# Weight residues of every fourth block by an adding transfer from HBM

## The chip, the cores and the metric

The kernel runs on one core of a Trainium2 chip. The metric is the device time of one execution in microseconds (us); lower is better.

## What is computed

The reference is one layer of a retention network with its MLP, for one sequence of 256 tokens, width 2048, all in float32:

```python
x = x + retention_mixer(rmsnorm(x, norm1), w_in, gain, w_out)     # 8 heads, DK = 256, DV = 512
x = x + square(relu(rmsnorm(x, norm2) @ w_up)) @ w_down           # width 8192
return rmsnorm(x, final_norm)

# the mixer: q, k, v, g = split(h @ w_in); q and k turned by rotary angles
# o = (q k^T * decay) v, chunk by chunk; y = head_norm(o) * silu(g) @ w_out
```

Nearly all the work is in products of activations with weights: w_in is 2048 x 12288, w_out 4096 x 2048, w_up 2048 x 8192, w_down 8192 x 2048, 268 MB in all. Each weight is read once.

## The kernel before

TensorE multiplies float32r numbers, which keep fewer bits than float32. So each weight w is split into two parts, `wh` (w rounded to float32r) and `wl = w - wh` (the residue), and so is each activation; a product is three passes, wh·xh + wl·xh + wh·xl, added up in PSUM.

Weights lie in HBM in contiguous blocks of 1 MB, 128 partitions by 2048 floats. `load_block` (L49) fetches one: a transfer on SP's queue into a `raw` tile (three buffers, L50 to L52), then for each of two halves of 1024 columns a cast to `wh` on ScalarE (L59) and a subtraction to `wl` on VectorE (L60). `wh` and `wl` have four buffers each (L55, L56), so the halves of two blocks. A half is two row tiles of 512 columns in w_qk, w_v, w_g and w_up, 1 row tile of 1024 columns in w_o and w_down. The first projection loads its four blocks row tile by row tile instead, with activations ahead of each (`lead`).

There are 256 blocks in this order. For each of 8 heads: gates (w_g, 4 blocks), queries and keys (w_qk, 4), values (w_v, 4). Then the output projection w_o in two halves of 16 blocks. Then twice (the MLP's two halves in width): w_up in 8 groups of 4 blocks, w_down in two halves of 16 blocks. `proj_cols` (L74) has weights stationary and is used for w_qk and w_up: a 512-column matmul with `wh` (L82) and a 256-column one with `wl` (L83). `proj_rows` (L89) has activations stationary and is used for the rest: per row tile, token block and 512 columns three matmuls of 512 columns (L97 with `wh`, L98 with `wl`, L101 with `wh`). In the last half of w_down the last four row tiles (the last two blocks) are kept and multiplied at the end, one accumulator after another (`late=4`, L116 to L127).

Other work of a head is put between blocks as fillers: `mix` of the head before (L268) and its `turn` (L294) behind the second block of gates and of queries, `scores` (L248) behind the second block of values. `mix` ends in a power on POOL (`rsqrt`, L141) for each token block. POOL has little else: sums of squares of x at the start, the transfers of x (L325) and of final_norm, the powers of the other norms.

Each engine works through its instructions in its own order. What the program's builder puts first is not always what the code names first: the casts of later blocks stand ahead of the work that waits for earlier matmuls.

Of the kernel before, what the change touches and what calls it, by code (L numbers as in the profile page):

```python
# [9 lines left out]
F32 = mybir.dt.float32  # L10
F32R = mybir.dt.float32r
AF = mybir.ActivationFunctionType
ALU = mybir.AluOpType
PSUM = bass.MemoryType.PSUM

P = 128
T = 256
D = 2048
# [7 lines left out]
EPS = 1e-6  # L26
# [3 lines left out]

@with_exitstack
def trunk_kernel(ctx: ExitStack, tc: tile.TileContext, io, out):
    """One retention layer and its squared-ReLU MLP.

    Every weight product is three float32r passes over exact 12-bit parts (w = wh + wl,
    x = xh + xl): wh*xh + wh*xl + wl*xh, accumulated in float32.
    """
    nc = tc.nc

    cp = ctx.enter_context(tc.tile_pool(name="cp", bufs=1))  # L40
# [3 lines left out]
    def bank(name):  # L44
        return ps.tile([P, 512], F32, tag="bank", name=name)

    # ---- weights: a block of 1 MiB, loaded whole and split in two halves; or, row tile by
    # row tile, with lead(row tile) before each ----
    def load_block(src, rows, cols, lead=None):  # L49
        raw = wp.tile([P, 2048], F32, tag="raw", name="raw", bufs=3)  # L50
        if lead is None:
            nc.sync.dma_start(raw, src)  # L52
        parts = []
        for s in range(2):
            wh = wp.tile([P, 1024], F32R, tag="wh", name="wh", bufs=4)  # L55
            wl = wp.tile([P, 1024], F32R, tag="wl", name="wl", bufs=4)  # L56
            r = raw[:, s * 1024 : (s + 1) * 1024]
            if lead is None:
                nc.scalar.copy(wh, r)  # L59
                nc.vector.tensor_sub(wl, r, wh.bitcast(F32))  # L60
            for k in range(rows // 2):
                sl = slice(k * cols, (k + 1) * cols)
                if lead is not None:
                    row = s * rows // 2 + k
                    lead(row)
                    nc.sync.dma_start(r[:, sl], src[:, row * cols : (row + 1) * cols])
                    nc.scalar.copy(wh[:, sl], r[:, sl])  # L67
                    nc.vector.tensor_sub(wl[:, sl], r[:, sl], wh[:, sl].bitcast(F32))  # L68
                parts.append((wh[:, sl], wl[:, sl]))
        return parts  # L70

    # weights stationary: acc[o][n, t] (xh) and acc[o][n, T + t] (xl) over the rows of w,
    # o = 0..3 blocks of 128 columns
    def proj_cols(src, xs, accs, fillers=()):  # L74
        for g in range(KT // 4):
            parts = load_block(src[g], 4, 512)
            for j, (wh, wl) in enumerate(parts):
                kt = 4 * g + j
                for o, acc in enumerate(accs):
                    c = slice(o * P, (o + 1) * P)  # L80
                    both = xs[:, kt].rearrange("p a t -> p (a t)")
                    nc.tensor.matmul(acc, wh[:, c], both, start=(kt == 0), stop=False)  # L82
                    nc.tensor.matmul(acc[:, :T], wl[:, c], xs[:, kt, 0, :], start=False, stop=(kt == KT - 1))  # L83
            for f in [f for at, f in fillers if at == g]:
                f()

    # activations stationary: accs[b][c][t, n] over nk row tiles, two token blocks; the last
    # `late` row tiles go to one accumulator after another, with done(b, c) behind each
    def proj_rows(blocks, per, xs, accs, nk, after=(), late=0, done=None, lead=None):  # L89
        nch = len(accs[0])  # L90
        kept = []
# [26 lines left out]
                if done:  # L118
                    done(b, c)

# [1 line left out]
    xs = cp.tile([P, KT, 2, T], F32R, tag="xs", name="xs")  # L122
    xr = cp.tile([P, KT, T], F32, tag="ys", name="xr", padded_shape=[P, VT * 2, T])
    norm1 = cp.tile([P, KT], F32, name="norm1")
# [6 lines left out]
    nc.vector.memset(ones, 1.0)  # L131
    nc.vector.memset(mhalf, -0.5)

    # while the first loads are under way: the activation table, and the tensor engine's clock
    warm = cp.tile([P, 1], F32, name="warm")
    nc.scalar.activation(warm, ones[:, 0:1], AF.Silu)
    pw = bank("pw")
# [1 line left out]
        nc.tensor.matmul(pw[:, :P], ones, ones, start=True, stop=True)  # L139

    def rsqrt(r, v):  # L141
        """r = v ** -0.5 for [P, 1] tiles."""
        nc.gpsimd.tensor_tensor(r, v, mhalf, op=ALU.pow)

    def split_scaled(dst, src, scale):
        """dst[:, 0] + dst[:, 1] = src * scale, scale [P, 1]."""
        nc.scalar.activation(dst[:, 0, :], src, AF.Copy, scale=scale)
        nc.vector.scalar_tensor_tensor(
            dst[:, 1, :], src, scale, dst[:, 0, :].bitcast(F32), op0=ALU.mult, op1=ALU.subtract
        )  # L150

    with tc.tile_pool(name="ap", bufs=1) as ap:
        # x transposed, times norm1, in two parts; sums of squares by token
        sq = ap.tile([P, 4, T], F32, name="sq")
        sqs = ap.tile([P, T], F32, name="sqs")
        cosr = ap.tile([P, T], F32, name="cosr")
# [3 lines left out]
        def load_x(k0, n):  # L160
            ks = slice(k0, k0 + n)
            nc.sync.dma_start(xr[:, ks], io["xT"][:, ks])
            for k in range(k0, k0 + n):
                split_scaled(xs[:, k], xr[:, k], norm1[:, k : k + 1])

        def lead_x(k):
            """x ahead of the first weights: row tile by row tile, then four at once."""
            if k < 4 or k % 4 == 0:
                load_x(k, 1 if k < 4 else 4)

# [30 lines left out]
            nc.vector.tensor_mul(cosr, cosr, rsrow)  # L201
            nc.vector.tensor_mul(sinr, sinr, rsrow)

# [1 line left out]
        st = {}  # L205

        def gates(h, after, lead=None):
# [38 lines left out]
            st["v"] = v  # L246

        def scores(h):  # L248
            """Decayed scores, keys on partitions: columns 0..255 keys 0..127, 256..383 keys 128..255."""
            qk = st["qk"]  # L250
            pst = bank("pst")
            for b in range(NB):
                q = slice(b * P, T)
                to = slice(0, T) if b == 0 else slice(T, T + P)
                for i in range(2):
                    nc.tensor.matmul(
                        pst[:, to], qk[:, 1, i, b * P : (b + 1) * P], qk[:, 0, i, q], start=(i == 0), stop=(i == 1)
                    )
            sd = ap.tile([P, 384], F32, tag="sd", name="sd")
            sh = ap.tile([P, 384], F32R, tag="sh", name="sh")  # L260
            sl = ap.tile([P, 384], F32R, tag="sl", name="sl")
            nc.vector.tensor_mul(sd[:, :T], pst[:, :T], dec[:, h])
            nc.vector.tensor_mul(sd[:, T:384], pst[:, T:384], dec[:, h, :P])
            nc.scalar.copy(sh, sd)
            nc.vector.tensor_sub(sl, sd, sh.bitcast(F32))
            st["s"] = sh, sl
# [49 lines left out]
                nc.sync.dma_start(dec, io["dec"])  # L316
            values(h, [(1, lambda h=h: scores(h))])

# [1 line left out]
        acc0 = [[bank("acc_o") for _ in range(2)] for _ in range(NB)]  # L320
        proj_rows(io["w_o"][0], 2, ys, acc0, VT, [(1, lambda: mix(H - 1)), (4, lambda: turn(H - 1))])

# [1 line left out]
    x = mp.tile([P, NB, D], F32, name="x")  # L324
# [4 lines left out]
    ms2 = mp.tile([P, NB], F32, name="ms2")  # L329
# [10 lines left out]
        )  # L340

    def partial_sum(b):
        """ms2 = the first three sums + D * EPS"""
        m = ms2[:, b : b + 1]
        nc.vector.tensor_scalar(m, ss[:, b, 0:1], ss[:, b, 1:2], D * EPS, op0=ALU.add, op1=ALU.add)
        nc.vector.tensor_add(m, m, ss[:, b, 2:3])
# [40 lines left out]
            nc.tensor.matmul(psr[:, b * P : (b + 1) * P], ones, dg2[:, b], start=True, stop=True)  # L387
        nc.vector.tensor_copy(rsrow2, psr[:, :T])

# [1 line left out]
    fnorm = mp.tile([P, D], F32, name="fnorm")  # L391
    nc.gpsimd.dma_start(fnorm, io["final_norm"])
    rs3 = mp.tile([P, NB], F32, name="rs3")
# [21 lines left out]
    for fh in range(2):  # L415
        hs = cp.tile([P, VT, 2, T], F32R, tag="ys", name="hs")
        for c in range(8):
            acc = [bank("acc_u") for _ in range(4)]
            proj_cols(io["w_up"][8 * fh + c], x1s, acc, [(1, second_norm)] if fh == 0 and c == 0 else ())
            for o in range(4):  # L420
                t = mp.tile([P, T], F32, tag="t", name="t", bufs=3)
                s = mp.tile([P, T], F32, tag="s", name="s", bufs=3)
# [7 lines left out]
        for half in range(2):  # L430
            acc = [[bank("acc_d") for _ in range(2)] for _ in range(NB)]
            last = fh == 1
            proj_rows(
                io["w_down"][fh][half], 2, hs, acc, VT,
                late=4 if last and half == 1 else 0,
                done=(lambda b, c: finish(b, half, c)) if last else (lambda b, c: add_residual(acc, half, b, c)),
# [1 line left out]


def _tables():  # L440
    """Rotary and decay tables: functions of the shapes alone."""
    f = np.float32
    inv = f(10000.0) ** (-np.arange(0, DK, 2, dtype=f) / f(DK))
    ang = np.arange(T, dtype=f)[None, :] * inv.astype(f)[:, None]
    cos, sin = np.cos(ang).astype(f), np.sin(ang).astype(f)
    lg = np.log1p(-np.exp2(-5.0 - np.arange(H, dtype=np.float64)))
    j, i = np.arange(P)[:, None], np.arange(T)[None, :]
    seen = (j // CHUNK) <= (i // CHUNK)
    dist = np.abs(i - j)
    dec = np.exp(lg[None, :, None] * dist[:, None, :]) * seen[:, None, :] * DK**-0.5  # L450
    return cos, sin, np.ascontiguousarray(dec.astype(f))


def _blocks(w, rows, cols):
    """[K, N] -> [N / cols, K / (128 rows), 128, rows, cols], each block contiguous."""
    k, n = w.shape
    w = w.reshape(k // (P * rows), rows, P, n // cols, cols).transpose(3, 0, 2, 1, 4)
    return np.ascontiguousarray(w).reshape(n // cols, k // (P * rows), P, rows * cols)
# [44 lines left out]
```

## Time and profile before

| | |
|---|---|
| median of 2 runs | 1492.38 us (1492.07 to 1492.69) |
| span of the profiled execution | 1491.0 us |
| TensorE (PE) busy | 1471.6 us, 99% |
| VectorE (DVE) busy | 852.9 us, 57% |
| ScalarE (ACT) busy | 675.8 us, 45% |
| GpSimd (POOL) busy | 40.3 us, 3% |
| read from HBM | 275.09 MB, 186 GB/s over the span |
| mean granted TensorE clock | 0.994 |

PE is a matmul, PEld a weight load on TensorE. A wait is written as the engine, line and tile that waited, an arrow, and what ended the wait. In a timeline, the figure in square brackets is the idle time of the engine before the instruction and what ended it. "SPq" and "POOL ... DMA_DIRECT2D" are issues of transfers. Ends of matmuls are modelled, so their starts are used for rates. A granted clock of 1.00 is 2.4 GHz, 0.50 is 1.2 GHz.

### The profile page before, as it was taken

To read this page: it belongs to the slowest core of one execution; us is meant where nothing else is said; L and a number is where in the kernel's file an instruction comes from. 1 tells how busy PE (TensorE), PEld (TensorE's weight loads), DVE (VectorE), ACT (ScalarE), POOL (GpSimd) and SP (SyncE) were. 2 spreads that over 40 slices of the span, in tenths; PEclk is the share of its full clock that TensorE was granted. 3 is DMA by queue.
4 is the path that set the end of the run, shared out by engine and by line. 5 is a ranking of instruction groups with operands and counts; after the bars stand their busy time and mean duration, and the time that the engine had idled before them with its cause. 6 is when DMAs were issued, how large, how long until landed. Compare 5 with 4: busy or idle time off the path is not lost.

```text
span 1491.0 us, 17881 instructions
## 1 busy us (share of the span) xinstructions
PE 1471.6 (99%) x7172; PEld 1233.2 (83%) x7172; DVE 852.9 (57%) x1099; ACT 675.8 (45%) x870; POOL 40.3 (3%) x48
## 2 busy tenths in 40 slices
PE   7999999999999999999999999999999999999997
PEld 5888888888888888888888888888888888888885
DVE  8656565656565656546466566544446566554645
ACT  5444444444444444434345455533334555443332
POOL 6000000000000000000000000000000000000000
PEclk8999999999999999999999999999999999999999
DMA  6654454454445445655555555555555555555552
GB/s 235 225 187 182 170 198 170 170 188 179 173 174 191 172 174 191 254 198 175 192 175 192 178 189 190 181 194 196 192 185 189 194 176 195 180 189 195 198 185 98
DMA packets 42260, 278.35 MB, mean 187 GB/s; under 512 B 5056, under 2 KB 5952, under 8 KB 9408
## 3 DMA queue, kind: packets, MB, share of 16 engines
q1 hardware_dynamic: 41616, 274.05, 52.2%
q0 software_dynamic: 416, 3.15, 0.5%
q8 instruction: 56, 0.92, 0.2%
q14 instruction: 28, 0.23, 0.0%
q10 hardware_dynamic: 144, 0.01, 0.0%
HBM read 275.09 MB, written 2.10 MB: 186 GB/s over the span
## 4 chain that ended last, share of the span: by engine, by line
PE 96%; DVE 1%; DMA 1%; issue 1%; ACT 0%; POOL 0%; SPq 0%; POOLq 0%; ACTq 0%; DVEq 0%
PE acc_u L82 16%; PE acc_qk L82 8%; PE acc_u L83 8%; PE acc_d L101 8%; PE acc_d L97 8%; PE acc_d L98 8%; PE acc_qk L83 4%; PE acc_v L101 4%; PE acc_v L97 4%; PE acc_v L98 4%; PE acc_o L97 4%; PE acc_o L101 4%; PE acc_g L101 4%; PE acc_o L98 4%; PE acc_g L98 4%; PE acc_g L97 4%
## 5 line engine op out<-in xcount | busy, mean ns | idle before, releaser
L60 DVE TENSOR_TENSOR wl<-raw,wh 128x1024 fp32r<-128x1024 f32 x504 | 615.6, 1224 | 600.9 <-ACT wh L59 600.8
L59 ACT CAST wh<-raw 128x1024 fp32r<-128x1024 f32 x504 | 529.8, 1051 | 703.6 <-PE acc_d L101 204.4
L82 PE MATMUL acc_u<-x1s,wh 128*128 128x512 f32 x1024 | 362.1, 398 | 0.0
L83 PE MATMUL acc_u<-x1s,wl 128*128 128x256 f32 x1024 | 287.8, 281 | 0.0
L82 PEld LDWEIGHTS acc_u<-x1s,wh 128*128 128x128 f32 x1024 | 192.5, 188 | 47.4
L97 PE MATMUL acc_d<-wh,hs 128*128 128x512 f32 x512 | 200.0, 391 | 0.0
L98 PE MATMUL acc_d<-wl,hs 128*128 128x512 f32 x512 | 199.9, 390 | 0.0
L83 PEld LDWEIGHTS acc_u<-x1s,wl 128*128 128x128 f32 x1024 | 192.2, 188 | 0.0
L82 PE MATMUL acc_qk<-xs,wh 128*128 128x512 f32 x512 | 182.1, 398 | 0.0
L101 PE MATMUL acc_d<-wh,hs 128*128 128x512 f32 x512 | 160.8, 393 | 0.0
L83 PE MATMUL acc_qk<-xs,wl 128*128 128x256 f32 x512 | 143.9, 281 | 0.0
L82 PEld LDWEIGHTS acc_qk<-xs,wh 128*128 128x128 f32 x512 | 96.3, 188 | 23.1
L98 PEld LDWEIGHTS acc_d<-wl,hs 128*128 128x128 f32 x512 | 96.1, 188 | 22.2 <-DVE wl L60 0.3
L101 PEld LDWEIGHTS acc_d<-wh,hs 128*128 128x128 f32 x512 | 96.2, 188 | 20.8
L97 PEld LDWEIGHTS acc_d<-wh,hs 128*128 128x128 f32 x512 | 96.2, 188 | 20.4
L98 PE MATMUL acc_g<-wl,xs 128*128 128x512 f32 x256 | 101.9, 398 | 7.5 <-DVE wl L68 7.5
L97 PE MATMUL acc_g<-wh,xs 128*128 128x512 f32 x256 | 101.9, 401 | 0.5 <-ACT wh L67 0.5
L101 PE MATMUL acc_g<-wh,xs 128*128 128x512 f32 x256 | 102.1, 399 | 0.0
L97 PE MATMUL acc_v<-wh,xs 128*128 128x512 f32 x256 | 100.8, 394 | 0.0
L101 PE MATMUL acc_v<-wh,xs 128*128 128x512 f32 x256 | 100.6, 393 | 0.0
L97 PE MATMUL acc_o<-wh,ys 128*128 128x512 f32 x256 | 100.6, 393 | 0.0
L98 PE MATMUL acc_o<-wl,ys 128*128 128x512 f32 x256 | 100.0, 391 | 0.0
(96 smaller groups left out, 1279.5 us busy)
## 6 DMA issues: line engine op xcount, KB each, us to landing
raw<-in_w_up SPq DMA_DIRECT2D x64, 1024.0 KB, 4.9
raw<-in_w_down SPq DMA_DIRECT2D x64, 1024.0 KB, 4.9
raw<-in_w_qk SPq DMA_DIRECT2D x32, 1024.0 KB, 4.9
raw<-in_w_v SPq DMA_DIRECT2D x32, 1024.0 KB, 4.9
raw<-in_w_o SPq DMA_DIRECT2D x32, 1024.0 KB, 4.9
raw<-in_w_g SPq DMA_DIRECT2D x28, 1024.0 KB, 4.9
raw<-in_w_g SPq DMA_DIRECT2D x16, 256.0 KB, 6.3
x<-in_x POOLq DMA_DIRECT2D x1, 2048.0 KB, 10.4
```

The costliest lines, as they stand in the source:

```text
L59: nc.scalar.copy(wh, r)
L60: nc.vector.tensor_sub(wl, r, wh.bitcast(F32))
L82: nc.tensor.matmul(acc, wh[:, c], both, start=(kt == 0), stop=False)
L83: nc.tensor.matmul(acc[:, :T], wl[:, c], xs[:, kt, 0, :], start=False, stop=(kt == KT - 1))
L97: nc.tensor.matmul(accs[b][c], xs[:, kt, 0, t], wh[:, n], start=(kt == 0), stop=False)
L98: nc.tensor.matmul(accs[b][c], xs[:, kt, 0, t], wl[:, n], start=False, stop=False)
L101: nc.tensor.matmul(accs[b][c], xs[:, kt, 1, t], wh[:, n], start=False, stop=(kt == nk - 1))
```

## The change

Every fourth call of `load_block` (the counter is raised in each call), unless it is one with `lead`, makes `wl` in another way. ScalarE writes a sign-turned copy of `raw` into `wl`; since `wl` is float32r, that copy is rounded as `wh` is, so it is -wh. Then a transfer on POOL's queue reads the same half of the block from HBM a second time and adds it onto `wl`, which becomes w - wh. VectorE's subtraction is left out there. The halves of the other blocks, the matmuls, buffers and loads stay. The diff also drops comments (not shown).

```diff
+    count = [0]
+
     def load_block(src, rows, cols, lead=None):
+        count[0] += 1
+        by_dma = lead is None and count[0] % 4 == 0
         raw = wp.tile([P, 2048], F32, tag="raw", name="raw", bufs=3)
         if lead is None:
             nc.sync.dma_start(raw, src)
...
             r = raw[:, s * 1024 : (s + 1) * 1024]
             if lead is None:
                 nc.scalar.copy(wh, r)
-                nc.vector.tensor_sub(wl, r, wh.bitcast(F32))
+                if by_dma:
+                    nc.scalar.activation(wl, r, AF.Copy, scale=-1.0)
+                    nc.gpsimd.dma_start(out=wl, in_=src[:, s * 1024 : (s + 1) * 1024], accum_op=ALU.add)
+                else:
+                    nc.vector.tensor_sub(wl, r, wh.bitcast(F32))
```

## Rows read from the trace of the kernel before

**Rows 1.** Page, engine totals (busy us, share, instructions) and chain that ended last.

```profile
PE 1471.6 (99%) x7172; PEld 1233.2 (83%) x7172; DVE 852.9 (57%) x1099; ACT 675.8 (45%) x870; POOL 40.3 (3%) x48
...
PE 96%; DVE 1%; DMA 1%; issue 1%; ACT 0%; POOL 0%; SPq 0%; POOLq 0%; ACTq 0%; DVEq 0%
```

**Rows 2.** List of waits: who waited for whom, us in total, times, longest us.

```profile
DVE wl L60 <- ACT wh L59: 600.8, 439, 2.3
...
PE acc_g L98 <- DVE wl L68: 7.5, 3, 4.0
...
PEld acc_d L98 <- DVE wl L60: 0.3, 1, 0.3
```

**Rows 3.** Timeline of TensorE and ScalarE, values of head 4: start, duration, instruction.

```profile
347.72 0.39 PE L97 MATMUL acc_v<-wh,xs 128*128 128x512 f32 x1
...
355.97 0.39 PE L97 MATMUL acc_v<-wh,xs 128*128 128x512 f32 x1
...
356.21 1.05 ACT L59 CAST wh<-raw 128x1024 fp32r<-128x1024 f32 x1 [1.69 <-PE acc_v L101]
```

**Rows 4.** Groups by line: busy us, mean ns of one, idle before, releaser.

```profile
L60 DVE TENSOR_TENSOR wl<-raw,wh 128x1024 fp32r<-128x1024 f32 x504 | 615.6, 1224 | 600.9 <-ACT wh L59 600.8
L59 ACT CAST wh<-raw 128x1024 fp32r<-128x1024 f32 x504 | 529.8, 1051 | 703.6 <-PE acc_d L101 204.4 <-PE acc_u L82 157.3 <-PE acc_o L101 102.2
```

**Rows 5.** Timeline of ScalarE and POOL around mix, in the gates behind head 3.

```profile
311.39 1.05 ACT L59 CAST wh<-raw 128x1024 fp32r<-128x1024 f32 x1 [1.70 <-PE acc_g L101]
...
315.39 0.72 ACT L291 ACTIVATE y<-y,rv 128x512 f32<-128x512 f32 x1 [2.96 <-DVE mv L285]
...
315.79 0.55 POOL L143 TENSOR_TENSOR rv<-ve,mhalf 128x1 f32<-128x1 f32 x1 [0.46 <-DVE ve L286]
```

**Rows 6.** Issue of x on POOL, and 615 to 616 (engines' busy us, PEclk, DMA, GB/s).

```profile
614.72 0.90 POOL L325 DMA_DIRECT2D x<-in_x  x1 [15.07 <-ACT ys L147]
...
615.00:616.00 1.00, 1.00 (x6) 0.80 (x5) 1.00 (x3) 0.05 (x2) 1.00 (x2) 1.00 0.00 0
```

**Rows 7.** One block's load: issue on SP, and stretches of its traffic (columns as rows 6).

```profile
321.35 0.33 SPq L52 DMA_DIRECT2D raw<-in_w_qk  x1
...
321.50:323.00 1.50, 1.50 (x8) 1.24 (x7) 0.17 (x1) 1.05 (x1) 0.00 (x0) 1.00 0.53 98
...
326.00:327.50 1.50, 1.50 (x11) 1.31 (x10) 1.23 (x1) 0.43 (x2) 0.00 (x0) 1.00 0.00 0
```

**Rows 8.** Transfers: the load queue's packets, MB and share; KB each, us to landing.

```profile
q1 hardware_dynamic: 41616, 274.05, 52.2%
...
raw<-in_w_down SPq DMA_DIRECT2D x64, 1024.0 KB, 4.9
...
x<-in_x POOLq DMA_DIRECT2D x1, 2048.0 KB, 10.4
```

**Rows 9.** Chain of work in order of time: TensorE's other work in the heads.

```profile
358.88 1.31 PE pst L256 x8
382.18 2.07 PE po L279 x9
406.54 0.87 PE pt L301 x8
```

**Rows 10.** Timeline of TensorE at the start, and stretches there (columns as rows 6).

```profile
10.58 0.50 PE L98 MATMUL acc_g<-wl,xs 128*128 128x512 f32 x1 [1.04 <-DVE wl L68]
...
28.46 0.51 PE L98 MATMUL acc_g<-wl,xs 128*128 128x512 f32 x1 [2.52 <-DVE wl L68]
...
29.98 0.63 PE L98 MATMUL acc_g<-wl,xs 128*128 128x512 f32 x1
...
33.38 0.39 PE L97 MATMUL acc_g<-wh,xs 128*128 128x512 f32 x1
...
12.00:14.00 2.00, 1.98 (x8) 0.97 (x6) 2.00 (x4) 2.00 (x5) 1.84 (x3) 1.00 1.03 409
...
31.00:33.00 2.00, 2.00 (x7) 1.52 (x6) 2.00 (x3) 0.65 (x1) 1.34 (x2) 0.50 0.24 45
```

## The prediction

> **What bounds the kernel now.** I read the page's engine totals and the chain of work that ended last first. The reader is to see that TensorE is busy for 99% of the span and makes up 96% of the chain [rows 1]: whatever makes it wait is added to the time, and work taken from another engine gives nothing back. Next the list of waits: TensorE's only waits for weight residues are 7.5 us in the first blocks and 0.3 us in a half of w_down [rows 2]. VectorE waits 600.8 us for ScalarE's casts [rows 2], and a cast waits 1.69 us for TensorE to give back a buffer [rows 3]; both engines have room. So the question is one of lateness alone: does the new transfer deliver `wl` before TensorE asks for it?
>
> **The time it has.** `wh` and `wl` have four buffers each, and a block uses two. A half that TensorE finishes gives its buffers to the half four further on, which TensorE reaches after the three halves between. In the values of head 4, 36 matmuls (three halves) take 355.97 - 347.72 = 8.25 us, so a half is 2.75 us and a matmul 0.229 us [rows 3]. The cast that wants the freed buffer starts 0.24 us later (356.21) [rows 3]. Cast and subtraction need 1.05 and 1.22 us [rows 4]: `wl` is there 2.5 us after the buffer comes free, 5.7 us early.
>
> **What goes and what comes.** The counter reaches 256 (w_qk, w_v, w_g and w_o 32 blocks each, w_up and w_down 64 each). The fourth is a `lead` block, so blocks 8, 12, ... 256 change: 63, with 126 halves. In each projection of four blocks that is the last one; in each half of w_o and w_down it is every fourth of 16.
> - VectorE loses 126 x 1.22 = 154 us, with no effect on the end: it waits more than that already [rows 2].
> - ScalarE gains 126 sign-turned copies. I price them by the cast, which has their shape: 126 x 1.05 = 132 us [rows 4]. A cast and a copy (2.1) fit into a half (2.75). What hides them is ScalarE's wait for TensorE's buffers [rows 3]; without it each would push the next cast by 1.05 us, still within 5.7.
> - `raw` is released 2.1 us behind the start of the cast, not 2.3, so the load that waits for it on SP's queue may start 0.2 us sooner. Nothing: `raw` has a third buffer.
> - POOL gets 126 issues, each waiting for its copy. Behind them in its queue stand only the small powers of the norms. Casts of block 3 of w_g, which the code places behind `mix`, already run ahead of it (311.39, before `y` at 315.39), so I take it that the issues do as well. If instead they stood behind the powers of `mix`, which end at 315.79 + 0.55 = 316.3 [rows 5], about 2.4 us before TensorE wants that block, some 3.5 us would be lost in each of 8 mixes: 28 us.
> - The queue gains 126 transfers of 512 KB. Here lies the cost.
>
> **The price of one transfer.** Nothing in the trace accumulates, so I bound it. *Start:* x's issue on POOL at 614.72 lasts 0.90 us, and the DMA engines carry nothing from 615 to 616 [rows 6]; I take first traffic at 1.4 us behind the issue. A load that SP issues at 321.35 averages 98 GB/s from 321.5 on [rows 7]; I take 0.5 us for it. *Work:* 274.05 MB keep 16 engines busy for 52.2% of 1491 us [rows 8], so a block of 1.05 MB takes 2.98 us of them. An add needs the old contents of `wl` too: 512 KB written stand for 0.5 MB read (1.49 us) if the second read is free, or for 1 MB read (2.98 us) if it goes through the same engines. *End:* the load of rows 7 carries its last bytes before 326 and lands at 321.35 + 4.9 = 326.25 [rows 7, 8]; I take 0.6 us. *From above:* x, 2 MB from POOL with loads beside it, lands after 10.4 us [rows 8]. I take 2.98 us, since the old contents must come from somewhere, and the nearest transfer of as many bytes read is a block's load.
>
> The Trainium skill ("Collectives: The Full Stack", section "The bandwidth ceiling: the fold count and why AG ≠ RS ≠ AR") says that an adding transfer is slower by its two source reads and not by its arithmetic. No run here shows that yet.
>
> **The sum.** Put the buffer of the block's first half free at 0. Cast and copy end at 0.24 + 2.1 = 2.3, POOL starts at 2.4, traffic starts at 3.8, 2.98 us of work end at 6.8, and the landing is at 7.4: 0.8 us ahead of 8.25. The second half is 2.75 us later, and the next block's load, released at 5.05, brings traffic from 5.6. From there the first transfer runs at half rate (1.2 us left, until 8.0, landed 8.6: up to 0.4 late). At 6.55, when the second starts, 0.7 (first) + 2.5 (load) + 2.98 = 6.2 us of work are queued; it ends near 12.5 and lands near 13.1, where TensorE wants it at 2.75 + 8.25 = 11.0. **Late by 2.1 us**; the first half's 0.4 is within that, as it moves the second's need along.
>
> By stage: w_o, w_down and w_up, 39 blocks without the last: 39 x 2.1 = 82. In the heads TensorE does other work between the blocks ahead: 1.31 us of scores, 2.07 of mix, 0.87 of turn [rows 9]. That leaves 0.8 in w_v (8 blocks, 6), nothing in w_g (7) and 1.2 in w_qk (8, 10). In the last block rows 28 to 31 are kept for the end: behind row 26, TensorE has only row 27 and six matmuls (2.75 + 1.37 = 4.1 us) before it wants the first half, which lands at 7.4: 3.3 late. The second half lands near 10.4 for a need at 8.1: 2.3 more, so 6 in all. Sum of waits: 82 + 6 + 10 + 6 = 104 us.
>
> **TensorE's clock.** After the wait of 2.52 us at the start matmuls come at 2.4 GHz at first, then the granted clock is 0.50 (1.2 GHz) between 31 and 33, though TensorE is busy [rows 10]. From 29.98 to 33.38 [rows 10] eight matmuls came 0.425 apart, not 0.229: 1.6 us lost. After the wait of 1.04 us the clock stays at 1.00 [rows 10]. A wait of 2.1 lies between; I charge half of 1.6 to each of the 39 blocks with about 2 us, 31 us. The bounds are 0 and 62. Against this execution: 1491 + 104 + 31 = 1626 in span, and 1.4 us more for the median (1492.4 against 1491.0): **1627 us**.
>
> **Rivals.**
> 1. *Hidden: not slower.* The old contents are read beside the stream, so a transfer has 1.49 us of work. Traffic from 3.8, at half rate beside a load 3.0 us, landing 7.4 against 8.25; the second half no later relative to its need. Only the last block waits, 2 to 4 us: **1492 to 1497**. For it: the load queue leaves the DMA engines idle 48% of the time [rows 8]. Against it: two transfers and a load overlap. It decides when work and queueing stay under 3.8 us per transfer. The Trainium skill ("DMA: Bandwidth & Descriptors", section "Anatomy of one DMA — SWDGE (gpsimd) path") gives about 2.0 us plus bytes over 436 GB/s for a transfer issued from POOL, for 512 KB an estimate of 3.2 us, and the time by it would be this rival's; by the same rule x would take 6.8 us, and the trace has 10.4, with loads beside it.
> 2. *Slow adding.* A transfer lands 10.4 us behind its issue, like x. Then each is late by 2.4 + 10.4 - 8.25 = 4.6 us in 39 blocks (179), by 3.7, 3.3 and 2.5 in w_qk, w_v and w_g (30 + 26 + 18), 9 at the end; and nearly each wait loses the clock, 60 x 1.6 = 96. Sum 358: **about 1850**. For it: reading, adding and writing back at SBUF is a round trip that no load makes. Against it: x is four times as large.
> 3. *POOL's order*: the 28 us above on top of the forecast, 1655; within its range.
>
> That VectorE's relief shows up as speed has no row for it: TensorE waits for `wl` in nothing but 8 us.
>
> **Chances.** Forecast (waits of 0.5 to 3.5 us in most blocks, 1525 to 1740): 0.45. Hidden, within 2%: 0.27. Slow adding, 1740 and more: 0.26, of it 0.12 above 1850. Faster: 0.02. The range from 1490 to 1850 leaves out about 0.13. About 2% (30 us, 0.5 us per changed block) is what a measurement of this kernel can tell from no change; so faster 0.02, within 0.27, slower 0.71.
>
> **What would show it.** Waits of TensorE at L98 and L83 for transfers, in 40 to 63 blocks, 2 us each, longest in w_down, w_o and w_up, least in w_g; a landing of 6 to 8 us for `wl` in the list of transfers; VectorE at about 700 us of busy time and ScalarE at about 810; the granted clock a few per cent lower. A landing under 5.7 us with no waits is rival 1; 10 us or more is rival 2. Waits in w_g alone would show POOL's order. The forecast is wrong in its mechanism if TensorE waits for ScalarE's casts, not for transfers, or if matmuls get longer without a wait.

## The result

| | before | changed |
|---|---|---|
| median of 2 runs | 1492.38 us | 1700.51 us (1696.16 to 1704.86) |
| ratio to before, 95% interval | | 1.1395 [1.1367, 1.1422] |
| span of the profiled execution | 1491.0 us | 1694.4 us |
| mean granted clock | 0.994 | 0.966 |

The change makes the kernel 14% slower: 208 us, against 135 us forecast. Engine totals and the load queues on the page of the changed kernel (engine, busy us, share, instructions; queue, packets, MB, share of 16 engines), for comparison with [rows 1] and [rows 8]:

```profile
PE 1534.2 (91%) x7172; PEld 1261.5 (74%) x7172; DVE 706.6 (42%) x973; ACT 795.6 (47%) x996; POOL 148.2 (9%) x174
...
q1 hardware_dynamic: 41616, 274.05, 45.4%
q0 software_dynamic: 18560, 69.21, 22.0%
...
PE 50%; DMA 35%; issue 10%; ACT 4%; DVE 1%; SPq 0%; POOL 0%; POOLq 0%; ACTq 0%; DVEq 0%
```

The span has grown by 203.4 us. Of this, 140.8 us are idle time of TensorE, which went from 1491.0 - 1471.6 = 19.4 to 1694.4 - 1534.2 = 160.2 us. The other 62.6 us are busy time, with the same 7172 matmuls. The mean granted clock accounts for about 49 of them: 0.034 of 1694.4 us are missing to the full clock, 57.6 us, against 0.006 of 1491.0 before, 8.9 us. What the other 14 us are isn't shown. The chain, 96% TensorE before, now runs through transfers for 35%. VectorE lost 146 us of work and gave nothing back.

Who waited, in the list of waits of the changed kernel, over the whole span (us, times, longest us); before, TensorE's only waits for residues were those of [rows 2], for VectorE:

```profile
PE acc_u L91 <- DMA wl<-in_w_up: 47.8, 17, 4.4
PE acc_d L106 <- DMA wl<-in_w_down: 39.8, 19, 3.8
PE acc_o L106 <- DMA wl<-in_w_o: 19.0, 8, 5.7
PE acc_v L106 <- DMA wl<-in_w_v: 14.1, 10, 2.6
PE acc_qk L91 <- DMA wl<-in_w_qk: 12.7, 8, 2.9
...
PE acc_g L106 <- DMA wl<-in_w_g: 6.3, 7, 1.7
```

These add up to 139.7 us in 69 waits, 2.0 us each: about one wait for each of the 63 changed blocks, and TensorE has no other new wait. (L91 and L106 are L83 and L98 of the kernel before, moved by the added lines.)

One changed block in w_up, in the timeline of the changed kernel (start, duration, engine, instruction, idle before):

```profile
931.98 0.86 POOL L66 DMA_DIRECT2D wl<-in_w_up  x1 [23.69 <-ACT wl L65]
933.46 1.06 ACT L65 ACTIVATE wl<-raw 128x1024 fp32r<-128x1024 f32 x1
934.54 0.33 SPq L56 DMA_DIRECT2D raw<-in_w_up  x1
934.80 0.86 POOL L66 DMA_DIRECT2D wl<-in_w_up  x1 [1.97 <-ACT wl L65]
944.09 0.39 PE L91 MATMUL acc_u<-x1s,wl 128*128 128x256 f32 x1 [2.79 <-DMA wl<-in_w_up]
```

The second half's copy, the two issues on POOL, and between them the load that this copy released (it ended at 933.46 + 1.06 = 934.52). By the list of transfers of these moments the first transfer lands 5.9 us behind its issue (937.9, in time), the load after 7.8 (942.3) and the second transfer after 9.2 (944.0). TensorE has wanted it since 941.3. The stretches of that block (busy us of PE, PEld, DVE, ACT, POOL with instruction counts, then granted clock, share of the DMA engines, GB/s) show the rest:

```profile
934.00:936.00 2.00, 2.00 (x13) 1.72 (x13) 0.00 (x0) 1.18 (x2) 0.86 (x1) 1.00 0.95 164
...
940.00:942.00 2.00, 1.30 (x8) 0.84 (x6) 0.46 (x1) 0.97 (x1) 0.00 (x0) 1.00 1.07 238
942.00:944.00 2.00, 0.00 (x0) 0.00 (x0) 1.23 (x1) 0.07 (x1) 0.00 (x0) 1.00 1.02 324
...
945.00:947.00 2.00, 2.00 (x9) 1.71 (x8) 0.02 (x1) 0.37 (x1) 0.00 (x0) 0.50 0.22 94
```

The DMA engines are full from 934 to 944. TensorE does nothing in the last two microseconds of that, and from 945 it is busy at 0.50 of its clock: the wait is paid for a second time, as at the start of the kernel before [rows 10]. Who had the DMA engines from 937 to 939 (load queue, then queue of the adding transfers: packets, MB, share):

```profile
q1 hardware_dynamic: 76, 0.62, 106.6%
q0 software_dynamic: 5, 0.00, 1.3%
```

The second transfer had been issued 2.2 us before that and got 1% of the engines: the load went first.

### The profile page after: what moved, and what is told of

Its sections match the earlier page's. It is cut to its first block, busy times and chain, and to the rows that moved or that the text cites. A ratio compares the mean times of both kernels' runs of the same rounds, so it can differ in the third digit from the quotient of the medians.

```text
span 1694.4 us, 18234 instructions
## 1 busy us (share of the span) xinstructions
PE 1534.2 (91%) x7172; PEld 1261.5 (74%) x7172; DVE 706.6 (42%) x973; ACT 795.6 (47%) x996; POOL 148.2 (9%) x174
## 3 DMA queue, kind: packets, MB, share of 16 engines
q1 hardware_dynamic: 41616, 274.05, 45.4%
## 4 chain that ended last, share of the span: by engine, by line
PE 50%; DMA 35%; issue 10%; ACT 4%; DVE 1%; SPq 0%; POOL 0%; POOLq 0%; ACTq 0%; DVEq 0%
PE acc_u L90 10%; DMA wl<-in_w_up 8%; DMA wl<-in_w_down 8%; PE acc_u L91 5%; DMA wl<-in_w_v 5%; PE acc_qk L90 4%; DMA wl<-in_w_o 4%; DMA wl<-in_w_g 4%; DMA wl<-in_w_qk 4%; ACT wl L65 3%; PE acc_d L106 3%; PE acc_d L105 3%; PE acc_o L106 3%; PE acc_d L109 3%; PE acc_v L106 2%
## 5 line engine op out<-in xcount | busy, mean ns | idle before, releaser
L68 DVE TENSOR_TENSOR wl<-raw,wh 128x1024 fp32r<-128x1024 f32 x378 | 461.5, 1224 | 740.4 <-ACT wh L63 740.2
L90 PE MATMUL acc_u<-x1s,wh 128*128 128x512 f32 x1024 | 384.2, 415 | 0.0
L91 PE MATMUL acc_u<-x1s,wl 128*128 128x256 f32 x1024 | 300.8, 294 | 47.8 <-DMA wl<-in_w_up 47.8
L91 PEld LDWEIGHTS acc_u<-x1s,wl 128*128 128x128 f32 x1024 | 203.8, 199 | 53.5 <-DMA wl<-in_w_up 53.3
L106 PE MATMUL acc_d<-wl,hs 128*128 128x512 f32 x512 | 206.4, 403 | 39.8 <-DMA wl<-in_w_down 39.8
L90 PEld LDWEIGHTS acc_u<-x1s,wh 128*128 128x128 f32 x1024 | 204.0, 199 | 50.1
L105 PE MATMUL acc_d<-wh,hs 128*128 128x512 f32 x512 | 204.1, 399 | 0.0
L65 ACT ACTIVATE wl<-raw 128x1024 fp32r<-128x1024 f32 x126 | 133.3, 1058 | 75.7 <-PE acc_d L106 28.6
L109 PE MATMUL acc_d<-wh,hs 128*128 128x512 f32 x512 | 164.4, 401 | 0.0
L91 PE MATMUL acc_qk<-xs,wl 128*128 128x256 f32 x512 | 145.5, 284 | 12.7 <-DMA wl<-in_w_qk 12.7
L106 PEld LDWEIGHTS acc_d<-wl,hs 128*128 128x128 f32 x512 | 98.4, 192 | 71.2 <-DMA wl<-in_w_down 50.2
L106 PE MATMUL acc_o<-wl,ys 128*128 128x512 f32 x256 | 104.2, 407 | 19.0 <-DMA wl<-in_w_o 19.0
L106 PE MATMUL acc_g<-wl,xs 128*128 128x512 f32 x256 | 102.8, 402 | 14.5 <-DVE wl L76 8.2
L106 PE MATMUL acc_v<-wl,xs 128*128 128x512 f32 x256 | 102.8, 402 | 14.2 <-DMA wl<-in_w_v 14.1
L109 PEld LDWEIGHTS acc_d<-wh,hs 128*128 128x128 f32 x512 | 98.5, 192 | 22.1
L91 PEld LDWEIGHTS acc_qk<-xs,wl 128*128 128x128 f32 x512 | 96.9, 189 | 15.7 <-DMA wl<-in_w_qk 15.3
L105 PE MATMUL acc_v<-wh,xs 128*128 128x512 f32 x256 | 101.9, 398 | 0.0
```

The source lines that it names most:

```text
L65: nc.scalar.activation(wl, r, AF.Copy, scale=-1.0)
L105: nc.tensor.matmul(accs[b][c], xs[:, kt, 0, t], wh[:, n], start=(kt == 0), stop=False)
L106: nc.tensor.matmul(accs[b][c], xs[:, kt, 0, t], wl[:, n], start=False, stop=False)
L109: nc.tensor.matmul(accs[b][c], xs[:, kt, 1, t], wh[:, n], start=False, stop=(kt == nk - 1))
```

## Experiments

Theory: the transfers are late, because each is worth twice its bytes to the DMA engines and because two of them and a load meet. Rivals: the way through POOL is slow, with or without adding; adding is slow by itself; the traffic as such slows the kernel.

**1. The same transfers, without adding** (e1_plain).

```diff
-nc.gpsimd.dma_start(out=wl, in_=src[...], accum_op=ALU.add)
+nc.gpsimd.dma_start(out=wl, in_=src[...])
```

> The changed kernel, but POOL's transfer overwrites wl with the weights and adds nothing, so that the residues of the changed blocks are wrong; copies, issues, bytes from HBM and waits stay. Theory (an adding transfer takes the DMA engines 2.9 us per 512 KB because it also reads the old contents, and that work beside a load is what makes it late): half the work, about 1.5 us per transfer, landing near 5 to 6 us, waits of TensorE under 40 us, time 1495 to 1540. Rival (the way through POOL and the second trip to HBM is what is long, adding costs little): landing stays near 8 us and the time near 1690.

Measured: 1542.25 us, ratio 1.0329 [1.0314, 1.0344]. The queue and the list of transfers of this run (KB, median us to landing):

```profile
q0 software_dynamic: 18560, 69.21, 14.6%
...
wl<-in_w_up POOLq DMA_DIRECT2D x32, 512.0 KB, 6.1
wl<-in_w_down POOLq DMA_DIRECT2D x32, 512.0 KB, 6.1
```

Adding costs 158 of the 208 us. The same bytes written keep the engines busy for 14.6% of 1537.4 us, where adding takes 22.0% of 1694.4: 224 against 373 us. The theory stands, but its range was missed by 2 us: plain transfers, too, are late by a little (35 us of waits) and cost 50 us. This speaks against rival 1 of the prediction: a plain transfer has no second read, and even it isn't hidden.

**2. Buffers of their own** (e2_own_buffers).

```diff
-wl = wp.tile([P, 1024], F32R, tag="wl", name="wl", bufs=4)
+if by_dma:
+    wl = wp.tile([P, 1024], F32R, tag="wd", name="wd", bufs=2)
+else:
+    wl = wp.tile([P, 1024], F32R, tag="wl", name="wl", bufs=3)
```

> The halves made by transfer get two wl buffers of their own and the others keep three, so a copy need not wait for the buffer that TensorE has only just left and its transfer can start as soon as raw has landed. All traffic stays. Theory (lateness alone costs, not traffic): nearly no waits, granted clock back to 0.99, 1492 to 1510. Rival (the DMA engines or SBUF are overloaded by 66 MB more, or the matmuls suffer from the writes): the time stays above 1600 though the transfers start earlier.

Measured: 1496.24 us, ratio 1.0025 [1.0016, 1.0034]. Engine totals, queue and transfers of this run:

```profile
PE 1470.2 (98%) x7172; PEld 1231.9 (82%) x7172; DVE 709.0 (47%) x973; ACT 790.3 (53%) x996; POOL 147.0 (10%) x174
...
q0 software_dynamic: 18560, 69.21, 26.2%
...
wd<-in_w_up POOLq DMA_DIRECT2D x32, 512.0 KB, 8.1
wd<-in_w_down POOLq DMA_DIRECT2D x32, 512.0 KB, 9.9
```

All traffic is there, and a transfer still takes 8 to 10 us. But it starts as soon as `raw` has landed (there are five buffers in all now, not four), TensorE's busy time is back at 1470.2 us, and 204 of the 208 us are gone. Lateness alone was the cost: neither the traffic nor the matmuls. It is still no faster than before, since what VectorE is spared bounds nothing.

**3 and 4. One half of the block only** (e3_one_half, e5_second_half).

```diff
-if by_dma:
+if by_dma and s == 0:        # e3_one_half; s == 1 in e5_second_half
```

> Only the first half of every fourth block is made by a transfer, the second by VectorE: 63 transfers, not 126. Theory (two adding transfers of 2.9 us and a load queue behind one another on the same engines): one transfer lands after 6 to 7 us where it was 8 to 10, waits fall by more than half, to 20 to 60 us, time 1520 to 1570. Rival (each transfer is long by itself, about 8 to 10 us, whatever is beside it): the waits at the first half stay, about 2.5 us in 50 blocks with the clock, time 1650 to 1700.

> Only the second half of every fourth block is made by a transfer, the first by VectorE: the 63 transfers that landed last in the changed kernel (9 to 10 us), without those in front of them. Theory A (the second is late because it queues behind the rest of the first): it lands after 6 to 7 us, time under 1530, so that the two halves' costs don't add up to the whole. Theory B (it is late because the next load starts just then and takes half of the engines): it still lands after 8 us or more, waits of 1 to 1.5 us in 40 blocks, time 1560 to 1650.

Measured: first halves alone 1513.24 us, 1.0139 [1.0122, 1.0156]; second halves alone 1568.39 us, 1.0511 [1.0496, 1.0527]. Waits of TensorE in the second of the two:

```profile
PE acc_u L91 <- DMA wl<-in_w_up: 23.6, 16, 1.8
...
PE acc_d L106 <- DMA wl<-in_w_down: 18.0, 16, 2.3
```

First halves alone came out below their range, with 12.6 us of waits, not 20 to 60; second halves alone within theory B's. Taken transfer by transfer, the first halves' land at nearly the same medians without and with the second (w_down 7.1 against 7.3 us, w_up 6.0 against 5.85): they are seldom what is late. The second halves' land after 7.9 to 8.1 us with nothing of their own kind in front of them, after 7.8 to 10.4 with it. So theory B is right in the main (the next load), and A adds to it: 21 + 76 = 97 us apart, 208 together.

**5. The next load held back** (e6_load_held).

```diff
 nc.gpsimd.dma_start(out=wl, in_=src[...], accum_op=ALU.add)
+if s == 1:
+    hold = wp.tile([P, 1], F32, tag="hold", name="hold", bufs=2)
+    nc.gpsimd.tensor_tensor(hold, r[:, 0:1], wl[:, 0:1].bitcast(F32), op=ALU.add)
```

> The changed kernel with one small POOL instruction per changed block that reads raw and wl behind the second transfer, so that raw, and with it the next load, is held until the second transfer has landed. Theory B (the load beside it makes the second transfer late): the second lands after 6 to 7 us, TensorE's waits fall below 50 us, time 1500 to 1560. Theory A (it is the first transfer in front of it): landing stays at 8 to 10 us and the time near 1700. Were the held load itself late, TensorE would wait for casts two blocks on instead.

Measured: 1512.69 us, ratio 1.0137 [1.0122, 1.0152]. Transfers, and the largest of TensorE's sums of waits for them:

```profile
wl<-in_w_up POOLq DMA_DIRECT2D x32, 512.0 KB, 5.7
wl<-in_w_down POOLq DMA_DIRECT2D x32, 512.0 KB, 7.5
...
PE acc_d L109 <- DMA wl<-in_w_down: 6.0, 7, 2.3
```

One small instruction per changed block takes away 188 of the 208 us, with every byte still moved. That the load beside the second transfer makes it late is shown by this. The held load itself is nowhere late: TensorE has no wait for a cast behind it.

**6. Adding from SBUF** (e7_from_sbuf).

```diff
-nc.gpsimd.dma_start(out=wl, in_=src[...], accum_op=ALU.add)
+nc.gpsimd.dma_start(out=wl, in_=r, accum_op=ALU.add)
```

> The transfers add raw from SBUF, not the block from HBM: 66 MB less from HBM; raw is held until they have landed, as in the run with the held load. If the second trip to HBM matters, this is quicker than that run by 20 us or more; if the engines' work (two reads, one write) alone matters, the two agree within 10 us.

Measured: 1507.97 us, ratio 1.0111 [1.0093, 1.0130], 5 us from the run with the held load. This edit holds `raw`, too. So where the load is held, the second trip to HBM (66 MB) costs no more than these 5 us, and the intervals of the two runs overlap. The engines' work stays: 23.1% of 1506.5 us in the queue of the transfers, against 25.2% of 1510.9. How much the second trip costs where the load is not held, no run shows.

**7. The copy behind the cast** (e4_copy_after_cast). In the changed kernel's timeline of ScalarE in w_down the copy runs ahead of the cast of the same half:

```profile
1140.70 1.06 ACT L65 ACTIVATE wl<-raw 128x1024 fp32r<-128x1024 f32 x1 [1.24 <-PE acc_d L106]
1141.66 1.04 ACT L63 CAST wh<-raw 128x1024 fp32r<-128x1024 f32 x1
```

`wl` comes free ahead of `wh`, which the last matmuls of a row tile still read (L109), and the copy needs nothing of the cast. The forecast had it behind. So:

```diff
-nc.scalar.activation(wl, r, AF.Copy, scale=-1.0)
+nc.scalar.activation(wl, wh.bitcast(F32), AF.Copy, scale=-1.0)
```

> The sign-turned copy reads wh, not raw, so that it must stand behind the cast, as the forecast had assumed; in the changed kernel w_down and w_o have it ahead of the cast, and POOL issues about 1.5 us earlier there. Theory (start times add to lateness one for one where queueing doesn't absorb them): 1.5 us more in some 24 to 40 blocks, 1725 to 1770. Rival (the engines' queue sets the landing, the start doesn't matter): within 10 us of 1700.

Measured: 1716.10 us, ratio 1.1490 [1.1450, 1.1531], 16 us above the changed kernel: neither the 25 to 70 us of the theory nor the 10 of the rival. The second transfer of w_down lands 8.8 us behind its issue, not 10.05. But the edit does a second thing: the copy no longer reads `raw`, so the cast alone releases the next load. In w_down SP issues it 1.36 us ahead of POOL's second issue, where in the changed kernel it came 0.67 us behind. So the run doesn't tell what a later start alone costs.

**8. The price by itself** (b1_bench, b2_pairs, b3_offsets). Three kernels with nothing but transfers.

> A kernel that computes nothing of the layer: chains of single 512 KB transfers, each waiting for the one before, six of a kind (from SP; from POOL into float32; from POOL into float32r; adding into float32; adding into float32r), then from POOL plain and adding beside loads of 1 MB that follow one another. Theory: from issue to landing 4 us for SP, 4.5 to 5 from POOL, 6 to 6.5 for adding (1.4 us more work), the type without effect; beside loads 6 to 7 plain and 9 to 11 adding. Rival (adding is a slow round trip): 8 to 10 us for adding even with nothing beside it.

> Nothing of the layer: pairs of 512 KB transfers from POOL, the second some 2.1 us behind the first, each pair waiting for the one before; plain and adding, alone and with a load of 1 MB issued by SP between the two. By theory A and B together: adding alone 5.5 us for the first and about 6.3 for the second (2.9 us of work each, 2.1 apart); with the load about 7 and 9, the load 8 to 9; plain 3.8 and 3.8 alone, 4 to 5 and 5 with the load.

> Nothing of the layer: one adding transfer of 512 KB from POOL and one load of 1 MB from SP, each pair waiting for the one before. The load's issue stands about 1 us before POOL's (e), about with it (f), about 1 us behind (g) and about 2 us behind (h); k is as f with the load in two transfers of 512 KB, with rows of 4 KB, not 8. Theory C (first come, first served): the adding transfer lands after about 8 us in e and f, and 5.5 to 6 in g and h, the load after 4.8 in e and f and 7 in g and h. Equal shares: both about 7 to 8 in e, f and g. If it is the load's longer rows that put it ahead, the adding transfer lands earlier in k than in f by 1 us or more.

List of transfers of the first: the loads (most with nothing beside them), plain from POOL, adding into float32 and into float32r, and adding beside loads:

```profile
ld<-in_w SPq DMA_DIRECT2D x40, 1024.0 KB, 4.8
...
plplain<-in_w POOLq DMA_DIRECT2D x6, 512.0 KB, 3.8
...
pladd<-in_w POOLq DMA_DIRECT2D x6, 512.0 KB, 5.5
pladdr<-in_w POOLq DMA_DIRECT2D x6, 512.0 KB, 5.5
...
besadd<-in_w POOLq DMA_DIRECT2D x6, 512.0 KB, 5.5
```

Adding costs 1.7 us over plain, not the 4 to 6 of a slow round trip: rival 2 of the prediction falls. All rows alone came out half a microsecond or more below the forecast (SP 3.5). The last row had been expected at 9 to 11. There the loads followed one another with one in flight, and each adding transfer was issued some 2 us ahead of the next load; the loads took the loss (5.8 to 6.75 us in place of 4.8). How long the DMA engines carry nothing behind an issue, for a plain transfer from SP at 5.42 and an adding one from POOL at 109.89 (last two figures: share of the DMA engines, GB/s):

```profile
5.42:6.30 0.88, 0.00 (x0) 0.00 (x0) 0.00 (x0) 1.00 0.00 0
109.89:111.40 1.51, 0.00 (x0) 0.00 (x0) 0.86 (x1) 1.00 0.00 0
```

POOL's adding transfer starts about 0.6 us later than SP's transfer.

In the second kernel the issues came closer than meant, 1.18 us apart (63.56 and 64.73). Adding pairs alone (paa, pab) and with a load issued by SP with the first (laa, lab, and the load, lal):

```profile
lal<-in_w SPq DMA_DIRECT2D x6, 1024.0 KB, 5.6
...
paa<-in_w POOLq DMA_DIRECT2D x6, 512.0 KB, 5.5
pab<-in_w POOLq DMA_DIRECT2D x6, 512.0 KB, 6.8
...
laa<-in_w POOLq DMA_DIRECT2D x6, 512.0 KB, 8.1
lab<-in_w POOLq DMA_DIRECT2D x6, 512.0 KB, 9.4
```

The load costs either transfer 2.6 us and loses 0.8 itself. It had been expected to land after 8 to 9 us, not 5.6. Beside plain pairs it loses nothing (4.8), and they land after 6.0 and 6.1 us, in place of 3.8 and 4.9. In the third kernel, by its timelines, the load's issue stood 1.3 us ahead of POOL's (e), level with it (f), 0.8 us behind (g) and 1.95 us behind (h); k is f with the load in two:

```profile
el<-in_w SPq DMA_DIRECT2D x6, 1024.0 KB, 5.2
fl<-in_w SPq DMA_DIRECT2D x6, 1024.0 KB, 5.7
gl<-in_w SPq DMA_DIRECT2D x6, 1024.0 KB, 7.5
hl<-in_w SPq DMA_DIRECT2D x6, 1024.0 KB, 7.3
...
ea<-in_w POOLq DMA_DIRECT2D x6, 512.0 KB, 6.8
fa<-in_w POOLq DMA_DIRECT2D x6, 512.0 KB, 8.2
ga<-in_w POOLq DMA_DIRECT2D x6, 512.0 KB, 7.3
ha<-in_w POOLq DMA_DIRECT2D x6, 512.0 KB, 5.5
ka<-in_w POOLq DMA_DIRECT2D x6, 512.0 KB, 8.7
```

Issued together, the load goes ahead and the adding transfer pays 2.7 us; issued 1.95 us later, the load pays 2.5 and the transfer nothing; at 0.8 us they share. So it is mostly first come, first served, with POOL's start some 0.6 us slower; at 1.3 us ahead and 0.8 us behind the landings lie between those of this theory and equal shares. Shorter rows of the load (k) don't help the transfer: the length of the load's rows is not why it wins. Each of these three kernels ran once.

**9. The load a little later** (e8_load_behind), and **that with the copy behind the cast** (e9_both).

```diff
+if s == 1:
+    mark = wp.tile([P, 1], F32, tag="mark", name="mark", bufs=2)
+    nc.scalar.copy(mark, wl[:, 0:1].bitcast(F32))
 nc.gpsimd.dma_start(out=wl, in_=src[...], accum_op=ALU.add)
+if s == 1:
+    hold = wp.tile([P, 1], F32, tag="hold", name="hold", bufs=2)
+    nc.gpsimd.tensor_tensor(hold, r[:, 0:1], mark, op=ALU.add)
```

> As the run with the held load, but raw is held only until POOL has issued the second transfer and done one small instruction that reads raw, some 1.5 us, not until the transfer has landed; a one-column copy on ScalarE stands ahead of the transfer so that this order is kept. The load and the transfer still overlap. Theory C (the engines serve what came first, and a load issued on SP behind the transfer gets ahead of it because its traffic starts 0.5 us after the issue, not 1.4): the second transfer now comes first and lands after 6 to 7.5 us, time 1510 to 1540. Theory B in its equal-shares form (both at half rate while they overlap): the second still lands after 8 us or more, time 1580 to 1690.

> The run with the load behind the issue, with the sign-turned copy made from wh and so behind the cast, as in the run with that order. In the former, w_up, w_qk and w_g lost nearly all their waits while w_down, w_o and w_v kept theirs (42, 19 and 17 us). There the copy runs ahead of the cast, and the first transfer's issue is only 1.3 us behind the load before it (2.8 in w_up). Theory (a backlog begun by that earlier load makes both transfers late): with later copies the second transfer lands after 6 to 7 us in every stage and the time is 1500 to 1535, so that two edits of which one alone cost 16 us are together worth 170 and more. Rival (row tiles of 1024 columns, or the stage, make the difference): w_down and w_o keep their waits, time 1600 to 1640.

Measured: 1618.32 us, 1.0822 [1.0782, 1.0863], and 1535.51 us, 1.0281 [1.0261, 1.0301]. TensorE's waits in the first of the two:

```profile
PE acc_d L112 <- DMA wl<-in_w_down: 42.4, 17, 3.6
...
PE acc_o L112 <- DMA wl<-in_w_o: 19.5, 7, 4.3
PE acc_v L112 <- DMA wl<-in_w_v: 16.8, 8, 3.4
...
PE acc_u L97 <- DMA wl<-in_w_up: 5.5, 7, 2.9
```

The first has a time within theory B's range, but by stage it is both theories: in w_up, w_qk and w_g the second transfer lands after 5.8 to 6.8 us, as C has it, in w_down, w_o and w_v after 9.4 to 10.1. The waits of w_up fell from 47.8 to 5.5 us, those of w_down stayed. In both stages the load now comes 1.1 us behind the second issue; what differs is the load before, 1.3 us ahead of the first issue in w_down, 2.8 in w_up, where the copy stands behind the cast. With the copies later everywhere (e9_both) the second transfer's median is 5.7 to 5.9 us in all stages but w_v (7.5), and w_down's waits are 8.6 us. So two edits, one of which alone cost 16 us and the other of which saved 82, save 165 together. This fits a backlog that begins with the load ahead; the rival, the stage or its row tiles, falls. The time is half a microsecond above its range. What makes the 27 us of waits that are left, in w_down, w_o and w_v, isn't shown.

## Why the prediction was right, and where it was off

The forecast was slower by 9%, 1627 us in a range of 1490 to 1850; measured 14%, 1700.5 us. Its mechanism holds: nothing gained on VectorE, TensorE waiting for the second transfer of a block beside the next load, a second loss on the clock. Both terms were too small: waits of 139.7 us for 104, and 62.6 us of busy time for 31. Step by step:

- **Engines' work per transfer**, taken as 2.98 us of all 16 for 512 KB written: (22.0% of 1694.4 - 0.5% of 1491.0) / 126 = 2.90 us. A block's load: 45.4% of 1694.4 over 261 MB-blocks, 2.94 us. An added half is worth a whole block. A plain half from POOL takes (14.6% of 1537.4 - 0.5% of 1491.0) / 126 = 1.72 us, so the reason given, the old contents, holds too. The rule of the Trainium skill ("Collectives: The Full Stack", section "The bandwidth ceiling: the fold count and why AG ≠ RS ≠ AR"), stated there for the reduce step between cores, is two source reads and so about twice the time. The trace agrees where a load is the measure (2.90 us, and a load of twice the bytes takes 2.94), and has less, 1.7 times, against a plain transfer from POOL. By the Trainium skill ("DMA: Bandwidth & Descriptors", section "Anatomy of one DMA — SWDGE (gpsimd) path") 512 KB would take an estimated 3.2 us. Measured alone, it is 3.8 us plain and 5.5 adding.
- **Start and end of a transfer**, taken as 0.5 us (SP), 1.4 us (POOL) and 0.6 us (end): the load of [rows 7] moves its first bytes 0.96 us behind its issue, and alone (experiment 8) the gap is 0.96 us for SP and 1.57 for an adding transfer from POOL; the end takes 0.3 to 0.4 us. The rows were read too finely for their stretches of 1.5 us. These errors are small and partly cancel.
- **First transfer**, put at 5.0 to 6.2 us behind its issue and on time: 5.7 to 8.55 us by stage. It was on time in most blocks: the experiment with first halves alone left 12.6 us of waits and 21 us of time. In the four stages with the copy ahead of the cast it took longer than the forecast, 7.2 to 8.55 us, but also began sooner.
- **Second transfer**, put at 7.95 us behind its issue: 9.2 in the block shown, 7.8 to 10.4 by stage. This is the term that was mis-sized. Two things were in it. The sum supposed that load and transfer share at equal rates, with nothing behind them. In the block shown the load went first (937 to 939), and before the second transfer was done the load after, issued at 940.49, already had 81.5% of the engines from 942.3 to 944, 1.4 us of their work. And in four of six stages the copy ran ahead of the cast, so that the first transfer met the tail of the load before. Waits were 139.7 us against 104: w_o, w_down and w_up 106.6 against 88 with the last block, w_v 14.1 against 6, w_qk 12.7 against 10, w_g 6.3 against 0. The order by stage was right. The cover by scores, mix and turn [rows 9] was there, but smaller than taken: 1.8 us of waits per block in w_v, 1.6 in w_qk and 0.9 in w_g, against 2.7 in w_o, w_down and w_up.
- **The clock**, charged with half of 1.6 us in 39 blocks, 31 us, with bounds of 0 and 62: about 49 us by the mean granted clock, 0.966 against 0.994. The 14 us of busy time beyond that were at nothing in the sum. In the run with second halves alone, 47 waits of 1.25 us each (58.7 in all) left the mean granted clock at 0.994, as before; the 15 us of busy time that came with them (1486.7 against 1471.6) are not the clock, and what they are stays open. By the timelines of the changed kernel, all 16 waits above 2.7 us came with a stretch at 0.50, and none of the 30 of 1.8 us or less did. In the run with the load behind the issue, four waits of 2.9 to 3.6 us came with none, so this is no rule. Charging half was a guess between two cases, and it fell short by 18 us.
- **ScalarE's order**: a step that failed, if a small one. The forecast took the order of the code for cast and copy.
- **POOL's order**: the powers of `mix` stand behind the second issue, as supposed, and TensorE never waited for them (ScalarE did, 6.0 us in 7 waits); rival 3 had no part.

With buffers of their own for the transfers the time came to what rival 1 (hidden) had forecast, 1496 us, but not for its reason: a transfer's work is 2.90 us, not its 1.49, and it still lands after 8 to 10 us. There it only starts early enough.

That the second transfer came out as near as it did has some luck in it: equal shares were wrong, but a queue that is worked off without a pause gives its last transfer the same end whoever goes first.

## What to carry to other kernels

Here a transfer that adds cost the DMA engines as much as a load of twice its bytes, and it saved nothing, because the engine that it relieved did not bound the kernel. What it adds is latency, 5.5 us here for 512 KB with nothing beside it and 8 to 10 with a load beside it: count the time from its start to its use, with the other transfers that the same event releases. If it must be, give its destination buffers that are free early (here 204 of 208 us), or hold back the load that would overtake it (188).

## What the runs showed of the hardware that I had not expected

- A load issued by SP level with a transfer issued by POOL is served ahead of it: 5.7 against 8.2 us, where alone they take 4.8 and 5.5. With the load 1.95 us later it is 7.3 against 5.5.
- The issue itself takes POOL 0.53 us for a plain transfer and 0.86 us for an adding one. The type written, float32 or float32r, made no difference.
- Costs did not add: first halves 21 us, second halves 76, both 208.
